# Scale steps, compressed scores and output products of a two-layer decoder trunk: which engine does them, and at which place in its order

## The chip, the cores and the metric

The kernel runs on one core of a Trainium2 chip. The metric is the device time of one execution in microseconds. A core has TensorE (PE: matmuls and transposes, with weight loads of their own), VectorE (DVE), ScalarE (ACT), GpSimd (POOL) and SyncE (SP, whose queue starts the transfers here). Each works through its own instruction stream in order; an instruction waits at its place until its operands are there, and what stands behind it on that engine waits too.

## The reference

Two layers over x of 1024 rows by 1024, each `x = x + (mixer(rmsnorm(x)) * silu(z)) @ w_out`, and a final rmsnorm. There are 16 heads of 64.

- Layer 0: full causal attention with a forget bias. `logits = q k^T / 8 + c[query] - c[key]`, with c the running sum of log sigmoids.
- Layer 1: three branches with 4 key and value groups, summed with gates. Compressed: 63 blocks of 32 keys (stride 16) go through a small MLP; `p_c` is the softmax over them, and `o_c = p_c v_c`. Chosen: the sums of p_c pick 8 of 16 blocks of 64 keys per query. Window: the last 512 keys.
- `o = g0 * o_c + g1 * o_s + g2 * o_w`, times silu(z), then `@ w_out`.

All is float32; the kernel keeps that precision by splitting operands into a high and a low part and adding up three products.

## The kernel before

**Order of the work.** The program is written as Python generators. `merge` interleaves a main generator (attention) with a filler (projections, output products) by costs that they yield and a ratio. That fixes the order in which instructions are traced. A scheduler then orders each engine's stream at compile time, by that order and by when it expects operands to be there, so an instruction traced late can be put earlier on its engine. `tc.keep_in_program_order(ins)` ties an instruction behind the last one traced before it on its engine.

**Layer 0.** `fox_main` runs score, softmax and value products for head pairs p = 0 to 7. `fox_fill` projects k, v, q, z of the next pair (`fox_k`, `fox_v`, `fox_q`, `fox_z`; each in two halves of 512 tokens, 8 steps of three matmuls a half). `early.step`, called once in each half, loads one piece of a later weight and has ACT sum its squares into a column of `sums`; columns 49 to 64 belong to `fox_w_out`. Power-of-two scales come out of such sums: `roots` (L187) copies the columns to bf16 on ACT, multiplies with ones on PE (tile `total_...`), and reduces and shifts exponents on DVE. `z_scale(p)` (L578) does it for z, `out_scales` (L226) for the output product: its first `roots` takes the square of the largest entry of `ao`, its second the sums of W_out. With the scale at hand `load_wout16` (L678) splits four rows of 128 of W_out into float16 halves: ACT the high part, DVE (L695) or POOL (L697, L698) the low part. `out_start0` then starts the output product in the filler. Where a pair's last super tile ends, its output is transposed and multiplied with z.

**Layer 1, projections and compressed branch.** `cmp_main` handles 16 units (`cmp_unit`, L1304: group g, half s, u: two tiles of 128 queries times four heads). The compressed keys `kcm` are held as high and low part side by side. Eight matmuls (L1310) write 128 columns each, high and low scores, into a tile `sc` of two banks, of which there is one buffer. DVE adds low part and mask (L1321, twice), then the high part (L1323), takes the minimum (L1324); ACT makes eight exponentials into `Pc` (L1326); DVE normalises, and for s = 1 sums over the heads (`pcs`, L1336) and picks blocks; POOL multiplies `Pc` in place with the gates (L1340). PE later transposes it (`ptc`, L1367). Meanwhile `nsa_fill` projects.

**Layer 1, attention.** `NsaSuper` is one head and one half s: eight `unit`s (y = 0 chosen, y = 1 window; four query tiles). A unit's scores (L1632) go to one of two buffers of two banks; DVE adds the mask and takes the minimum `m` in one instruction (L1640); for the window, DVE turns it into the exponent's offset (L1642); ACT makes the exponentials (L1643). Window probabilities are split on POOL (L1646, L1647) and transposed by DMA; chosen ones are transposed on PE (L1665) and split by ACT and DVE (L273, L274). `close` (L1713) transposes a pair's output, adds the compressed branch (L1723) and multiplies with the scale `ready["c", p]` and z (L1724), all on DVE; ACT and POOL split the product (L1731). The filler is `nsa_zs`: z projections (`nsa_z`), with `nz_scale(p - 1)` (L1448) four steps into the next, `limits` (L1432) once, then `out_scales`, the split of W_out and `out_start`. `out_rest` ends the program.

Of the kernel before, what the change touches and what calls it, by code (L numbers as in the profile page):

```python
# [25 lines left out]
GR = 4  # L26
# [15 lines left out]
def tile_fox_nsa(ctx, tc, a, out):  # L42
# [28 lines left out]
    tri = consts.tile([P, P], F32, name="tri")  # L71
    eps = consts.tile([P, 1], F32, name="eps")
# [153 lines left out]
    def out_scales(ao, cols, name, u, pool):  # L226


        V.tensor_reduce(u[:, 8:9], ao, AX.X, OP.max)
        V.tensor_tensor(u[:, 9:10], u[:, 8:9], u[:, 8:9], OP.mult)  # L230
        r = roots(u[:, 9:10], ((0, 1),), f"{name}a", pool)
        w = roots(cols, ((0, cols.shape[1]),), f"{name}w", pool)
        V.tensor_scalar(u[:, 10:11], r[:, 1], 2.0 ** 70, None, OP.mult)
        V.tensor_scalar(u[:, 11:12], w[:, 1], 2.0 ** 69, None, OP.mult)
        V.tensor_scalar(u[:, 0:8], ao, u[:, 10:11], None, OP.mult)
        V.tensor_scalar(u[:, 0:8], u[:, 0:8], u[:, 11:12], None, OP.mult)
        V.tensor_scalar(u[:, 10:11], r[:, 0], 2.0 ** 58, None, OP.mult)
        V.tensor_scalar(u[:, 11:12], w[:, 0], 2.0 ** 57, None, OP.mult)
        V.tensor_tensor(u[:, 10:11], u[:, 10:11], u[:, 11:12], OP.mult)
        return u[:, 0:8], u[:, 10:11]  # L240
# [323 lines left out]
    def fox_z(p, w, halves=(1, 0)):  # L564
# [3 lines left out]
        zs["q"] = zq = sb[0].tile([P, 6], F32, tag="zq", bufs=3, name=f"zq_{p}")  # L568
# [9 lines left out]
    def z_scale(p):  # L578
# [3 lines left out]
        V.tensor_tensor(zq[:, 2:3], zq[:, 0:1], zq[:, 1:2], OP.add)  # L582
# [5 lines left out]
    early = Squares(sa, [(a["nsa_w"][i][:, 4 * x:4 * x + 4, :], 2 * n + x)  # L588
                         for n, i in enumerate((*range(12), *range(20, 28))) for x in range(2)]
                    + row_sets(a["fox_w_out"], 512, 49)  # L590
# [5 lines left out]
    def fox_fill():  # L596
        for p in range(8):
            if p >= 2:
                yield lambda p=p: ("scored", p - 2) in ready
            yield from k0 if p == 0 else fox_k(p)  # L600
# [12 lines left out]
            else:  # L613
                wq, wz = next_w(), next_w()
                yield from fox_z(p, wz)
                yield from fox_q(p, wq, (1,))
                z_scale(p)
                rows0 = load_wout16(hp, "fox_w_out", 1, 200)
                yield next(rows0)
                last_q = fox_q(p, wq, (0,))  # L620
                for _ in range(4):
                    yield next(last_q)
                assert len(early.at) == 1 and not early.items
                ready["wscale"], ready["undo"] = out_scales(ao[0], sums[:, 49:65], "o0", un0, sb[0])
# [836 lines left out]
    def nsa_z(p, w, halves=(1, 0)):  # L1461
        if p == 0:
            limits()
# [411 lines left out]
```

## Time and profile before

| what | value |
|---|---|
| median of three runs | 1459.39 us (1457.80 to 1462.68) |
| profiled execution | 1460.85 us |
| its span, first to last instruction | 1458.8 us |
| mean granted clock of TensorE | 0.986 |
| busy: PE, DVE, ACT, POOL | 1364.8, 1119.4, 915.7, 588.2 us |

Busy time of PE counts overlapping matmuls once. The profile's windows give each engine's busy time in a stretch of the span, and the granted clock there (1.00 is full speed). In rows of waits the first engine and line waited for the second, with the total in us, the number of times and the longest. A bracket behind a timeline row is the idle time of the engine just ahead, and what ended it.

### The profile page before, as it was taken

The numbers are of one execution on the slowest core, as the hardware profiler recorded it, in microseconds if no ns is written. First come the engines' busy times: TensorE is split into PE (matmuls) and PEld (weight loads), VectorE is DVE, ScalarE is ACT, GpSimd is POOL, SyncE is SP. The second block draws the span as 40 slices with busy tenths as digits, with TensorE's granted clock in tenths as the row PEclk, the third lists the DMA queues.
The fourth block names the chain that finished last, engine by engine and source line by source line (L and its number), as shares of the span: only waits on it lengthen the run. The fifth ranks groups of instructions, "written<-read, shape, count | busy, mean of one in ns | idle before, by whom it ended". The sixth has DMA issues, their size and how long they took to land. (4 is left out here: it accounts for less than half of the span.)

```text
span 1458.8 us, 30392 instructions
## 1 busy us (share of the span) xinstructions
PE 1364.8 (94%) x10499; PEld 928.3 (64%) x10499; DVE 1119.4 (77%) x3018; ACT 915.7 (63%) x2328; POOL 588.2 (40%) x785
## 2 busy tenths in 40 slices
PE   5999999999999989989999987979999999988998
PEld 4878888888888745445545543446666767666643
DVE  6586777787877798586757667878989999989834
ACT  5376667776766665155554575657778787777512
POOL 2242433434243261221204455246756676654500
PEclk9999999999999999999999999999999999999999
DMA  5388898988989999354655447454767776785534
GB/s 202 91 176 183 198 186 184 215 184 191 193 196 186 230 235 207 115 174 139 188 179 149 130 123 159 117 140 95 135 151 169 128 177 119 146 182 108 106 109 144
DMA packets 414922, 234.72 MB, mean 161 GB/s; under 512 B 334448, under 2 KB 372656, under 8 KB 414768
## 3 DMA queue, kind: packets, MB, share of 16 engines
q1 hardware_dynamic: 414768, 232.78, 67.8%
q8 instruction: 83, 1.36, 0.4%
q14 instruction: 71, 0.58, 0.1%
HBM read 120.31 MB, written 28.38 MB: 102 GB/s over the span
## 5 line engine op out<-in xcount | busy, mean ns | idle before, releaser
L1632 PE MATMUL S_n<-nk,nq 128*128 128x320 f16 (+5 forms) x768 | 155.9, 316 | 20.7 <-DVE m_n L1640 16.1
L766 ACT ACTIVATE P<-P,m 128x512 f32<-128x512 f32 (+1 forms) x192 | 116.3, 606 | 54.6 <-DVE m L757 53.4
L1647 POOL TENSOR_TENSOR hl_n<-P_n,hl_n 128x640 f16<-128x640 f32 (+4 forms) x128 | 144.3, 1127 | 10.0
L737 POOL TENSOR_TENSOR Bd<-B,tri 128x128 f32<-128x128 f32 x128 | 61.5, 496 | 201.0 <-DVE m L757 190.1
L768 DVE SCALAR_TENSOR_TENSOR hl<-P,hl 128x512 f16<-128x512 f32 (+1 forms) x192 | 116.2, 621 | 26.4 <-ACT hl L767 25.1
L1646 POOL CAST hl_n<-P_n 128x640 f16<-128x640 f32 (+4 forms) x128 | 75.1, 587 | 126.9 <-ACT P_n L1643 102.4
L1643 ACT ACTIVATE P_n<-P_n,m_n 128x640 f32<-128x640 f32 (+7 forms) x128 | 98.5, 770 | 31.5 <-DVE m_n L1640 30.8
L1643 ACT ACTIVATE P_n<-P_n,m_n,units 128x640 f32<-128x640 f32 (+4 forms) x128 | 100.1, 782 | 24.5 <-DVE m_n L1642 23.8
L1632 PEld LDWEIGHTS <-nq 128*128 128x128 f16 x768 | 71.9, 98 | 67.9 <-issue 28.6
L273 ACT ACTIVATE pth_n<-ptp_n 128x512 f16<-128x512 f32 (+1 forms) x160 | 85.2, 545 | 44.4 <-PE ptp_n L1665 43.8
L274 DVE SCALAR_TENSOR_TENSOR ptl_n<-ptp_n,pth_n 128x512 f16<-128x512 f32 (+1 forms) x160 | 99.8, 633 | 11.8 <-ACT pth_n L273 10.0
L1665 PE MATMUL ptp_n<-ident,P_n 128*128 128x128 f32 x576 | 96.1, 285 | 5.8 <-ACT P_n L1643 1.6
L767 ACT ACTIVATE hl<-P 128x512 f16<-128x512 f32 (+1 forms) x192 | 92.5, 513 | 1.6 <-DMA pT<-hl 0.2
L1640 DVE CUSTOM_DVE_ANT_0 P_n<-S_n,wmask 128x640 f32<-128x640 f32 (+4 forms) x128 | 83.2, 650 | 6.4 <-PE S_n L1632 6.0
L1665 PEld LDWEIGHTS ptp_n<-ident,P_n 128*128 128x128 f32 x576 | 66.7, 144 | 29.8 <-DVE ptl_n L274 10.2
L183 ACT ACTIVATE sq<-sq,zg 128x512 f32<-128x512 f32 (+2 forms) x73 | 59.5, 815 | 25.3 <-DMA sq<-in_fox_w_out_dram 14.7
L1673 PE MATMUL O_n<-nv,pth_n 128*128 128x64 f16 x576 | 72.3, 194 | 0.3
L1674 PE MATMUL O_n<-nv,pth_n 128*128 128x64 f16 x576 | 72.2, 194 | 0.0
L97 ACT ACTIVATE h_n<-xr 128x512 f32<-128x512 f32 x32 | 20.0, 626 | 81.6 <-DVE xr L1765 39.2
L1640 DVE CUSTOM_DVE_ANT_0 P_n<-S_n,bias,units 128x640 f32<-128x640 f32 (+1 forms) x64 | 68.8, 1075 | 3.0 <-PE S_n L1632 2.8
L1675 PE MATMUL O_n<-nv,ptl_n 128*128 128x64 f16 x576 | 69.2, 194 | 0.1
L748 PE MATMUL S<-KH,Q 128*128 128x512 f32 (+1 forms) x192 | 65.2, 355 | 0.7 <-DVE m L757 0.7
(520 smaller groups left out, 4727.1 us busy)
## 6 DMA issues: line engine op xcount, KB each, us to landing
sq<-in_nsa_w_dram SPq DMA_DIRECT2D x40, 256.0 KB
B<-cD SPq DMA_DIRECT2D x16, 512.0 KB
nq<-qD SPq DMA_DIRECT2D x64, 128.0 KB
x<-in_x_dram SPq DMA_DIRECT2D x8, 512.0 KB
wst_k<-in_fox_w_dram SPq DMA_DIRECT2D x8, 512.0 KB
wst_v<-in_fox_w_dram SPq DMA_DIRECT2D x8, 512.0 KB
wst_q<-in_fox_w_dram SPq DMA_DIRECT2D x8, 512.0 KB
KH<-KH SPq DMA_DIRECT2D x32, 128.0 KB
```

Of the source, the lines that this page charges most:

```text
L273: A.activation(hi[:, 0:n], pt[:, 0:n], AF.Copy, scale=scale)
L274: V.scalar_tensor_tensor(lo[:, 0:n], pt[:, 0:n], scale, h, OP.mult, OP.subtract)
L766: A.activation(L[:, 0:n], L[:, 0:n], AF.Exp, bias=init, scale=-1.0, accum_out=self.lr[:, col + c:col + c + 1])
L767: A.activation(hi[:, cs], L[:, 0:n], AF.Copy, scale=UP)
L768: V.scalar_tensor_tensor(lo[:, cs], L[:, 0:n], UP, hi[:, cs], OP.mult, OP.subtract)
L1632: T.matmul(ps[:, b, 0:w], self.q[x][:, qi * P:(qi + 1) * P], k[:, k0 + b * w:k0 + b * w + w], start=(x == 0), stop=(x == 1))
L1640: V.tensor_tensor_reduce(dst, src, mk, 1.0 if y else unit, 3e38, OP.add, OP.min, m)
L1643: A.activation(L, L, AF.Exp, bias=m, scale=minus if y else -1.0, accum_out=self.l[:, y, qi:qi + 1])
L1646: G.tensor_copy(hl[:, 0:n], L)
L1647: G.tensor_tensor(hl[:, n:2 * n], L, hl[:, 0:n], OP.subtract)
L1665: T.transpose(pt[:, (x + i) * P:(x + i + 1) * P], L[:, kb * P - k0:(kb + 1) * P - k0], ident)
L1673: T.matmul(o, hi, v[:, 0:64], start=first, stop=False)
```

## The change

Seven things are done.

1. `out_scales` is cut into `w_scale` (sums of W_out), `out_scales1` (largest entry, squared by ACT, multiplied with ones on PE) and `out_scales2` (the rest, on DVE). In layer 0 `w_scale` runs at p = 3; for this the pieces of `fox_w_out` are the first in the list of `early`. In layer 1 it runs in `limits2`.
2. The first DVE instruction of `z_scale`, `nz_scale`, `limits2` and `out_scales2` is kept in program order; `limits` is cut in two, with the second part four steps into the next half.
3. For p = 7 of layer 0 the order is z half 1, q half 1, loads of W_out, z half 0, two steps of q half 0, `z_scale`, `out_scales1`, four steps, `out_scales2`, the rest. Of that half of W_out, DVE does two of four rows whole (`vrows`); the other halves stay as they were.
4. `cmp_unit`: sixteen matmuls of 64 columns add high and low part in one bank (two buffers); one DVE instruction adds the mask; exponentials stay in `L`, and POOL writes `Pc` from it.
5. The offset of the window's minimum is made by ACT (Identity, with bias `lnup`).
6. `nz_scale` has ACT scale z in place, and `close` multiplies with z on POOL.
7. In layer 1 the yields around `out_scales` are 1500 and 2500 in place of 2000.

The diff, with little of its context:

```diff
@@ -69,6 +69,8 @@
     tri = consts.tile([P, P], F32, name="tri")
+    lnup = consts.tile([P, 1], F32, name="lnup")
+    G.memset(lnup, LNUP)
     eps = consts.tile([P, 1], F32, name="eps")
@@ -223,21 +225,34 @@
-    def out_scales(ao, cols, name, u, pool):
+    late_on = tc.keep_in_program_order
+
+    def w_scale(cols, name, pool):
+
+
+        r = roots(cols, ((0, cols.shape[1]),), name, pool)
+        V.tensor_scalar(r[:, 2], r[:, 0], 2.0 ** 57, None, OP.mult)
+        V.tensor_scalar(r[:, 3], r[:, 1], 2.0 ** 69, None, OP.mult)
+        return r
+
+    def out_scales1(ao, u, name, pool):
...
         V.tensor_reduce(u[:, 8:9], ao, AX.X, OP.max)
-        V.tensor_tensor(u[:, 9:10], u[:, 8:9], u[:, 8:9], OP.mult)
-        r = roots(u[:, 9:10], ((0, 1),), f"{name}a", pool)
-        w = roots(cols, ((0, cols.shape[1]),), f"{name}w", pool)
-        V.tensor_scalar(u[:, 10:11], r[:, 1], 2.0 ** 70, None, OP.mult)
-        V.tensor_scalar(u[:, 11:12], w[:, 1], 2.0 ** 69, None, OP.mult)
+        tb = pool.tile([P, 1], BF16, name=f"sb_{name}")
+        A.activation(tb, u[:, 8:9], AF.Square)
+        pt = ps_t(f"total_{name}")
+        T.matmul(pt[:, 0:1], ones, tb, start=True, stop=True)
+        return pt
+
+    def out_scales2(ao, u, pt, w):
+        late_on(V.tensor_copy(u[:, 8:9], pt[:, 0:1]))
+        half_root(u, 8)
+        V.tensor_scalar(u[:, 10:11], u[:, 10:11], 2.0 ** 70, None, OP.mult)
         V.tensor_scalar(u[:, 0:8], ao, u[:, 10:11], None, OP.mult)
-        V.tensor_scalar(u[:, 0:8], u[:, 0:8], u[:, 11:12], None, OP.mult)
-        V.tensor_scalar(u[:, 10:11], r[:, 0], 2.0 ** 58, None, OP.mult)
-        V.tensor_scalar(u[:, 11:12], w[:, 0], 2.0 ** 57, None, OP.mult)
-        V.tensor_tensor(u[:, 10:11], u[:, 10:11], u[:, 11:12], OP.mult)
-        return u[:, 0:8], u[:, 10:11]
+        V.tensor_scalar(u[:, 0:8], u[:, 0:8], w[:, 3], None, OP.mult)
+        V.scalar_tensor_tensor(u[:, 11:12], u[:, 9:10], 2.0 ** 58, w[:, 2], OP.mult, OP.mult)
+        ready["wscale"], ready["undo"] = u[:, 0:8], u[:, 11:12]
@@ -565,7 +580,9 @@
             ao.append(sb[0].tile([P, 8], F32, name="ao0", bufs=1))
-        zs["q"] = zq = sb[0].tile([P, 6], F32, tag="zq", bufs=3, name=f"zq_{p}")
+        if "q" not in zs:
+            zs["q"] = sb[0].tile([P, 6], F32, tag="zq", bufs=3, name=f"zq_{p}")
+        zq = zs["q"]
         for half in halves:
@@ -579,15 +596,14 @@
         zq = ready["zt", p]["q"]
-        V.tensor_tensor(zq[:, 2:3], zq[:, 0:1], zq[:, 1:2], OP.add)
+        late_on(V.tensor_tensor(zq[:, 2:3], zq[:, 0:1], zq[:, 1:2], OP.add))
         half_root(zq, 2)
...
-    early = Squares(sa, [(a["nsa_w"][i][:, 4 * x:4 * x + 4, :], 2 * n + x)
+    early = Squares(sa, row_sets(a["fox_w_out"], 512, 49) + [(a["nsa_w"][i][:, 4 * x:4 * x + 4, :], 2 * n + x)
                          for n, i in enumerate((*range(12), *range(20, 28))) for x in range(2)]
-                    + row_sets(a["fox_w_out"], 512, 49)
                     + [(a["nsa_w_g"].rearrange("(k p) c -> p k c", p=P), 40)], 512, 1)
@@ -597,6 +613,8 @@
                 yield lambda p=p: ("scored", p - 2) in ready
+            if p == 3:
+                wr0 = w_scale(sums[:, 49:65], "o0w", sb[0])
             yield from k0 if p == 0 else fox_k(p)
@@ -612,22 +630,25 @@
                 wq, wz = next_w(), next_w()
-                yield from fox_z(p, wz)
+                yield from fox_z(p, wz, (1,))
                 yield from fox_q(p, wq, (1,))
+                rows0 = load_wout16(hp, "fox_w_out", 1, 200, 2)
+                yield next(rows0)
+                yield from fox_z(p, wz, (0,))
+                last_q = fox_q(p, wq, (0,))
+                for _ in range(2):
+                    yield next(last_q)
                 z_scale(p)
-                rows0 = load_wout16(hp, "fox_w_out", 1, 200)
-                yield next(rows0)
-                last_q = fox_q(p, wq, (0,))
+                pt = out_scales1(ao[0], un0, "o0", sb[0])
                 for _ in range(4):
                     yield next(last_q)
-                assert len(early.at) == 1 and not early.items
-                ready["wscale"], ready["undo"] = out_scales(ao[0], sums[:, 49:65], "o0", un0, sb[0])
+                out_scales2(ao[0], un0, pt, wr0)
                 yield from last_q
...
                 ready["o7"] = hp.tile([P, NT, 2, P], F16, tag="h11", name="o7_0")
-                yield from out_start0(load_wout16(hp, "fox_w_out", 0, 200))
+                yield from out_start0(load_wout16(hp, "fox_w_out", 0, 200, 0))
@@ -675,7 +696,7 @@
-    def load_wout16(pool, src, half, pace, gp=True):
+    def load_wout16(pool, src, half, pace, vrows):
@@ -691,7 +712,7 @@
                 A.activation(w[:, 0, k, cs], lo[:, k, cs], AF.Copy, scale=sc)
-                if c or not gp:
+                if c or k < vrows:
                     V.scalar_tensor_tensor(w[:, 1, k, cs], lo[:, k, cs], sc, w[:, 0, k, cs], OP.mult, OP.subtract)
@@ -955,7 +976,7 @@
     psP = tc.alloc_tile_pool(name="psP", bufs=2, space=PSUM, reuse_waits="tile")
-    psC = tc.alloc_tile_pool(name="psC", bufs=1, space=PSUM, reuse_waits="tile")
+    psC = tc.alloc_tile_pool(name="psC", bufs=2, space=PSUM, reuse_waits="tile")
@@ -1304,40 +1325,38 @@
         kcm = ready["kcm"]
-        sc = psC.tile([P, 2, 512], F32, tag="sc", name=f"sc_{nm}")
+        sc = psC.tile([P, 4, 2, 64], F32, tag="sc", name=f"sc_{nm}")
         for y in range(2):
             for r in range(4):
-                T.matmul(sc[:, y, r * P:(r + 1) * P], Q[r][:, (2 * u + y) * P:(2 * u + y + 1) * P],
-                         kcm[:, g].rearrange("p a c -> p (a c)"), start=True, stop=True)
-        sc = sc.rearrange("p y (r a c) -> p y r a c", r=4, a=2)
+                for x in range(2):
+                    T.matmul(sc[:, r, y], Q[r][:, (2 * u + y) * P:(2 * u + y + 1) * P], kcm[:, g, x],
+                             start=(x == 0), stop=(x == 1))
         t0 = 4 * s + 2 * u
-        L = pc[0].tile([P, 2, 4, 64], F32, tag="cL", bufs=2, name=f"cL_{nm}")
+        L = pc[0].tile([P, 4, 2, 64], F32, tag="cL", bufs=2, name=f"cL_{nm}")
         Pc = pc[0].tile([P, 2, 4, 64], F32, tag="cP", bufs=4, name=f"cP_{nm}")
         sm = pc[0].tile([P, 3, 8], F32, tag="cs", bufs=3, name=f"cs_{nm}")
-        L8 = L.rearrange("p y r c -> p (y r) c")
-        P8 = Pc.rearrange("p y r c -> p (y r) c")
+        L8 = L.rearrange("p r y c -> p (r y) c")
         uc = ready["uc"]
-        for y in range(2):
-            V.scalar_tensor_tensor(L[:, y], sc[:, y, :, 1, :], uc, cmask[:, t0 + y, None, :].to_broadcast([P, 4, 64]),
-                                   OP.mult, OP.add)
-        V.scalar_tensor_tensor(L8, sc.rearrange("p y r a c -> p (y r) a c")[:, :, 0, :], uc, L8, OP.mult, OP.add)
+        mk = cmask[:, t0:t0 + 2].rearrange("p y c -> p (y c)")[:, None, :].to_broadcast([P, 4, 128])
+        V.scalar_tensor_tensor(L.rearrange("p r y c -> p r (y c)"), sc.rearrange("p r y c -> p r (y c)"), uc, mk,
+                               OP.mult, OP.add)
         V.tensor_reduce(sm[:, 0, :], L8, AX.X, OP.min)
         for i in range(8):
-            A.activation(P8[:, i, :], L8[:, i, :], AF.Exp, bias=sm[:, 0, i:i + 1], scale=-1.0, accum_out=sm[:, 1, i:i + 1])
+            A.activation(L8[:, i, :], L8[:, i, :], AF.Exp, bias=sm[:, 0, i:i + 1], scale=-1.0, accum_out=sm[:, 1, i:i + 1])
         V.reciprocal(sm[:, 2, :], sm[:, 1, :])
+        ri = sm[:, 2, :].rearrange("p (r y) -> p r y", y=2)
         if t0 == 0:
-            V.tensor_scalar(sm[:, 2, 0:4], sm[:, 2, 0:4], crow, None, OP.mult)
-        ri = sm[:, 2, :].rearrange("p (y r) -> p y r", y=2)
+            V.tensor_scalar(ri[:, :, 0], ri[:, :, 0], crow, None, OP.mult)
         gc = gates[:, t0:t0 + 2, 12 * g:12 * g + 12:3]
         if s:
-            V.tensor_tensor(P8, P8, sm[:, 2, :, None].to_broadcast([P, 8, 64]), OP.mult)
+            V.tensor_tensor(L8, L8, sm[:, 2, :, None].to_broadcast([P, 8, 64]), OP.mult)
             pcs = pc[0].tile([P, 2, 65], F32, tag="pcs", bufs=2, name=f"pcs_{nm}")
             G.memset(pcs[:, :, 0:1], 0.0)
-            V.tensor_reduce(pcs[:, :, 1:65], Pc.rearrange("p y r c -> p y c r"), AX.X, OP.add)
+            V.tensor_reduce(pcs[:, :, 1:65], L.rearrange("p r y c -> p y c r"), AX.X, OP.add)
         else:
-            V.tensor_tensor(ri, ri, gc, OP.mult)
-            gc = ri
-        G.tensor_tensor(Pc, Pc, gc[:, :, :, None].to_broadcast([P, 2, 4, 64]), OP.mult)
+            V.tensor_tensor(ri, ri, gc.rearrange("p y r -> p r y"), OP.mult)
+            gc = ri.rearrange("p r y -> p y r")
+        G.tensor_tensor(Pc, L.rearrange("p r y c -> p y r c"), gc[:, :, :, None].to_broadcast([P, 2, 4, 64]), OP.mult)
         if s:
@@ -1429,7 +1448,7 @@
-    def limits():
+    def limits1():
@@ -1437,30 +1456,37 @@
             T.matmul(pt[:, g:g + 1], va[:, g, :], ones[:, 0:1], start=True, stop=True)
+        return pt
+
+    def limits2(pt):
         b = pers.tile([P, 2, GR], F32, name="limits")
-        V.tensor_scalar(b[:, 0], pt[:, 0:GR], ready["units"][2], None, OP.mult)
+        late_on(V.tensor_scalar(b[:, 0], pt[:, 0:GR], ready["units"][2], None, OP.mult))
         V.scalar_tensor_tensor(b[:, 0], vinv, 2.0 ** 16, b[:, 0], OP.mult, OP.add)
...
         ready["limits"] = b[:, 1]
+        ready["w1"] = w_scale(late.out, "o1w", pers)
...
         zq = ready["zt", p]["q"]
-        V.tensor_tensor(zq[:, 2:3], zq[:, 0:1], zq[:, 1:2], OP.add)
+        late_on(V.tensor_tensor(zq[:, 2:3], zq[:, 0:1], zq[:, 1:2], OP.add))
         half_root(zq, 2)
...
         V.tensor_scalar(ao1[:, p:p + 1], zq[:, 7:8], 0.5, None, OP.mult)
-        ready["c", p] = zq[:, 6:7]
+        for half in (1, 0):
+            z = ready["zt", p][half]
+            A.activation(z, z, AF.Copy, scale=zq[:, 6:7])
+        ready["c", p] = True
...
         if p == 0:
-            limits()
+            sums_v = limits1()
         zs = ready.setdefault(("zt", p), {})
@@ -1472,6 +1498,11 @@
                 nz_scale(p - 1)
+            if not half and not p:
+                for _ in range(4):
+                    yield next(steps)
+                assert not late.items and not late.at
+                limits2(sums_v)
             yield from steps
@@ -1482,18 +1513,20 @@
             if p == 6:
-                rows0 = load_wout16(h1, "nsa_w_out", 1, 400, False)
+                rows0 = load_wout16(h1, "nsa_w_out", 1, 400, 4)
                 yield next(rows0)
...
             yield from nsa_z(p, zw[p])
-        assert not late.items and not late.at
-        yield 2000
+        yield 1500
         nz_scale(7)
-        ready["wscale"], ready["undo"] = out_scales(ao1, late.out, "o1", pers.tile([P, 12], F32, name="un1"), pers)
+        un1 = pers.tile([P, 12], F32, name="un1")
+        pt = out_scales1(ao1, un1, "o1", pers)
+        yield 2500
+        out_scales2(ao1, un1, pt, ready["w1"])
         yield from rows0
         ready["o7"] = h1.tile([P, NT, 2, P], F16, tag="h11", name="o7_1")
-        yield from out_start(load_wout16(h1, "nsa_w_out", 0, 400, False))
+        yield from out_start(load_wout16(h1, "nsa_w_out", 0, 400, 4))
@@ -1639,7 +1672,7 @@
             if y:
-                V.tensor_scalar(m, m, unit, LNUP, OP.mult, OP.add)
+                A.activation(m, m, AF.Identity, bias=lnup, scale=unit)
             A.activation(L, L, AF.Exp, bias=m, scale=minus if y else -1.0, accum_out=self.l[:, y, qi:qi + 1])
@@ -1721,7 +1754,7 @@
             V.scalar_tensor_tensor(o, pt, vinv[:, self.g:self.g + 1], o, OP.mult, OP.add)
-            V.scalar_tensor_tensor(o, o, ready["c", p], ready["z", p, s][s], OP.mult, OP.mult)
+            G.tensor_tensor(o, o, ready["z", p, s][s], OP.mult)
             if p == 7:
```

## The prediction

> **What bounds the kernel now.** I read the page's engine totals first, then the waits of TensorE, then windows by stage, then the timeline around the longest gaps.
>
> ```profile
> span 1458.8 us, 30392 instructions
> PE 1364.8 (94%) x10499; PEld 928.3 (64%) x10499; DVE 1119.4 (77%) x3018; ACT 915.7 (63%) x2328; POOL 588.2 (40%) x785
> ```
>
> TensorE (PE) is the bound as a whole: 94.0 of 1458.8 us are without a matmul. The change takes no matmul work away, so it can only win from those 94 us, and from slow-clock time behind gaps. The windows say where they lie (columns: window, length, busy time of PE, weight loads, DVE, ACT, POOL, granted clock, DMA share, GB/s):
>
> ```profile
> 505.00:515.00 10.00, 7.08 (x50) 5.40 (x50) 8.40 (x34) 6.58 (x18) 1.13 (x3) 0.83 1.12 287
> 515.00:545.00 30.00, 23.70 (x141) 11.87 (x138) 28.43 (x68) 19.61 (x47) 22.46 (x24) 0.94 0.96 235
> 800.00:950.00 150.00, 133.86 (x744) 71.33 (x742) 108.16 (x267) 92.32 (x349) 67.40 (x97) 0.99 0.50 130
> 950.00:975.00 25.00, 18.10 (x88) 9.46 (x89) 17.02 (x59) 14.16 (x29) 11.87 (x14) 0.91 0.58 166
> 1116.00:1166.00 50.00, 48.05 (x623) 34.14 (x621) 46.08 (x128) 39.42 (x93) 35.08 (x42) 1.00 0.81 168
> 1300.00:1335.00 35.00, 27.22 (x338) 20.11 (x336) 30.43 (x94) 28.52 (x62) 14.95 (x19) 0.90 0.60 132
> ```
>
> PE is idle 9.2 us where layer 0 ends (505 to 545), 16.1 in the compressed branch (800 to 950), 6.9 where attention of layer 1 starts (950 to 975), 2.0 per 50 us inside attention, 7.8 where its output scales are made (1300 to 1335). The waits name what ended those gaps (us in total, times, longest):
>
> ```profile
> PE S_n L1632 <- DVE m_n L1640: 16.1, 24, 2.8
> PE ptc_c L1367 <- POOL cP L1340: 6.5, 5, 2.2
> PE ptc_c L1367 <- POOL pcs L1335: 5.4, 2, 3.3
> PE S_n L1632 <- DMA nq<-qD: 3.7, 1, 3.7
> PE sc L1310 <- DVE cL L1323: 3.5, 1, 3.5
> PE y L257 <- POOL wo_fox_w_out L698: 3.5, 3, 1.6
> POOL cP L1340 <- DVE pcs L1336: 17.2, 3, 7.0
> ```
>
> **Part A, the end of layer 0.** The timeline, with the idle time ahead in brackets:
>
> ```profile
> 504.73 0.18 PE L196 MATMUL total_o0a<-sb_o0a,ones 128*128 128x1 bf16 x1
> 509.33 0.17 PE L196 MATMUL total_o0w<-sb_o0w,ones 128*128 128x16 bf16 x1 [2.92 <-ACT sb_o0w L194]
> L698 POOL TENSOR_TENSOR wo_fox_w_out<-wos_fox_w_out,wo_fox_w_out x8: 1154/1314/1532, 515.7 to 537.5; 128x512 f16<-128x512 f32 x8
> L697 POOL TENSOR_SCALAR wos_fox_w_out<-wos_fox_w_out,un x8: 692/918/1230, 514.8 to 536.8; 128x512 f32<-128x512 f32 x8
> L695 DVE SCALAR_TENSOR_TENSOR wo_fox_w_out<-wos_fox_w_out,un,wo_fox_w_out x8: 737/772/1650, 515.3 to 541.0; 128x512 f16<-128x512 f32 x8
> ```
>
> The sum over the squares of fox_w_out (total_o0w) holds the in-order PE for 2.92 us, because its last squares come last in the list of loads. The diff puts them first and sums them at p = 3: the 2.92 us go. The window 505 to 515 runs at a clock of 0.83, which on 7.08 us of matmuls is 1.2 us more; that goes with the gap. The new sum at p = 3 can wait for its own squares: between 0 (total_o0a did not wait) and 2.9; near the first, since 17 squares should be done by then: +0.5. The Square and matmul of out_scales1 stand where total_o0a stood, four steps of the last query projection ahead of their use; a wait there is again between 0 and 2.9, and I take 0, as the row shows. Behind that wait every matmul would queue.
>
> Of the first half of W_out, two of four rows go from POOL to DVE. POOL loses 2 x (0.92 + 1.31) = 4.5 us, DVE gains 2 x 0.77 = 1.5. PE waited 3.5 us on these POOL instructions; the later rows also come earlier, so I take 2.0 of it. DVE is busy 28.43 of 30 us in that window, and scores queue behind the added 1.5: between 0 and 1.5, I take 0.6. Four weight DMAs (128 x 1024 each) are issued one projection sooner on SP's queue, past the load of one set of squares and the transposes of the attention ahead; if they delay those, ACT waits in its square and its exponentials queue behind it. The moved loads took the same queue before, so I take 0. Bounds for all of A: -8 (both waits and both slow stretches gone) and +3 (one new 2.9 us wait). Sum: -2.9 - 1.2 - 2.0 + 0.5 + 0.6 = **-5.0**. What is late next is the DVE itself.
>
> **Part B, pinned scale steps.** In the timeline of DVE and PE at the start of attention:
>
> ```profile
> 960.73 0.16 DVE L1452 TENSOR_TENSOR nzq<-nzq 128x1 f32<-128x1 f32 x1 [6.12 <-ACT nz L1477]
> 962.79 1.84 PE L1632 MATMUL S_n<-nk,nq 128*128 128x384 f16 x8 [2.82 <-DVE m_n L1640]
> ```
>
> The scheduler put the first instruction of nz_scale(0) ahead of the mask set-up and the first scores; it held the in-order DVE 6.12 us for ACT, and PE then ran out of score banks. The pin puts it behind what was traced before it, so the first minima can start some 5 us sooner. The window's idle PE time is 6.9 us, so the gain is between 0 (something else is late: ACT is idle only 10.8 of 25 us) and 6.9; I take **-4.0**, a little more than the named gap of 2.82, as the following short waits of the same kind lie in the same window. The later nz_scale steps did not wait so long; pinning them costs nothing as long as their use is a pair of heads later. limits split in two, and w_scale of layer 1 (one bf16 copy on ACT, one matmul, some 0.15 us instructions on DVE), lie under the projection of z of p = 0.
>
> **Part C, the compressed scores.** Rows by line (minimum/median/maximum ns), and two pieces of the timeline:
>
> ```profile
> L1321 DVE SCALAR_TENSOR_TENSOR cL<-sc,rc,cmask x32: 431/474/484, 822.6 to 942.6; 128x256 f32<-128x256 f32 x32
> L1323 DVE SCALAR_TENSOR_TENSOR cL<-sc,rc,cL x16: 699/750/753, 823.5 to 943.4; 128x512 f32<-128x512 f32 x16
> L1336 DVE TENSOR_REDUCE pcs<-cP x8: 1023/1039/1056, 834.8 to 948.7; 128x128 f32<-128x512 f32 x8
> 910.74 0.62 PE L1310 MATMUL sc<-kcm,nq 128*128 128x128 f16 x8 [3.55 <-DVE cL L1323]
> 1104.22 0.19 PE L1673 MATMUL O_n<-nv,pth_n 128*128 128x64 f16 x1
> 1104.54 0.19 PE L1675 MATMUL O_n<-nv,ptl_n 128*128 128x64 f16 x1
> ```
>
> On PE, 8 matmuls of 128 columns become 16 of 64, each with its own weight load. The eight take 0.62 us. Twelve 64-column matmuls start within 1104.22 to 1104.54, 0.029 apart, so sixteen take some 0.47 plus a tail of 0.16: nothing lost. On DVE, per unit, 2 x 0.474 + 0.750 becomes one of about 0.750: 0.95 less, 16 units, 15.2 us in all. The exponentials now stay in L, so POOL's product with the gates no longer waits until the sum pcs (1.04 us, 8 units) has read its operand; that wait is most of POOL's 17.2 us. So the chain that ends in the transposes ptc is 0.95 to 2.0 us shorter per unit. Seven waits there cost PE 6.5 + 5.4 us, 1.7 each, so at most 11.9 go; the second score bank takes away the 3.5 us wait of sc. Upper bound 15.4, lower bound 0 (the interleaving with projections fixes the pace, and the next projection's operand may be late instead). I take a third, **-5.0**, as DVE and ACT are busy only 72% and 62% there, which leaves room, but ptc waits also hang on ACT's eight exponentials, which stay.
>
> **Part D, attention of layer 1.** Groups by shape and line:
>
> ```profile
> L1642 DVE TENSOR_SCALAR m_n<-m_n,units 128x1 f32<-128x1 f32 x128 | 26.3, 206 | 1.2
> L984 ACT ACTIVATE zr<-pn_qr,roots_early 128x1 f32<-128x1 f32 x6 | 1.6, 259 | 4.2 <-DVE spl_qr L1151 4.2
> L1724 DVE SCALAR_TENSOR_TENSOR no<-no,nzq,nz 128x512 f32<-128x512 f32 x16 | 14.1, 879 | 0.1
> L1731 POOL TENSOR_TENSOR ot_n<-no,ot_n 128x512 f16<-128x512 f32 x14 | 16.2, 1160 | 2.9 <-ACT ot_n L1730 2.9
> L1232 ACT ACTIVATE nvT<-nvT,nvsc x8: 706/712/723, 852.0 to 889.4; 128x512 f32<-128x512 f32 x8
> L1454 DVE TENSOR_SCALAR nzq<-nzq x8: 141/153/155, 965.8 to 1306.5; 128x1 f32<-128x1 f32 x8
> L1455 DVE TENSOR_TENSOR nzq<-nzq,limits x8: 148/474/883, 968.8 to 1309.4; 128x1 f32<-128x1 f32 x8
> ```
>
> DVE loses 128 steps on the minima (26.3 us) and 16 products (14.1 us): 40.4 us of the some 430 between 960 and 1390, from 92% busy (46.08 of 50) to about 83%. ACT gains 128 x 0.259 = 33.2 us (L984 is the nearest form: Identity on one column with a bias from SBUF) and two scalings of z per pair, 16 x 0.712 = 11.4 us: 44.6 us, from 79% (39.42 of 50) to about 89%. POOL gains 16 x 1.16 = 18.6 us, from 70% to 74%. So the load changes sides rather than going away: the minimum's step stays in the chain from score to exponential, 0.259 in place of 0.206, and what queues behind a late minimum is now ACT's queue, the copies pth among it, not DVE's. PE is idle 2.0 of 50 us, 430/50 x 2.0 = 17 us over the stage, 5 to 7 of them already in part B. Bounds: -9 (most of what is left) and +22 (two thirds of ACT's 33.2 exposed). I take **-1.5**, near the first end, since DVE is the fuller engine before and PE's waits name DVE's minimum. In the last pair POOL's 1.16 in place of DVE's 0.88 would add 0.3 us; the output products of row tiles 4 to 7, which need only the other half, cover it.
>
> L1455 and L1454 show that DVE instructions reading two SBUF tensors wait for something: both work on one column, one takes 148 to 883 ns, the other 155 at most. The Trainium skill, "SBUF — State Buffer", section "Who interferes with whom", says why: DVE and GpSimd share a port pair as an exclusive lock, and a DVE instruction with two SBUF inputs blocks against a GpSimd instruction that reads SBUF. By that rule the move to POOL has a price: six per cent more POOL time, and as much more of such waits. By the rows it takes one such DVE instruction (L1724) away for each product added, so the sum would be the same within 0.5 us. The trace agrees with the rule.
>
> **Part E, the scales of layer 1's output.** out_scales2 comes 2000 cost units of filler later, so the split of W_out starts 2 to 4 us later; the 3.7 us wait in the window 1300 to 1335 is one for a DMA of queries, which the change does not touch. Between -2 and +3; I take 0.
>
> **Sum.** -5.0 - 4.0 - 5.0 - 1.5 + 0 = -15.5 us against the profiled execution, 1460.85 us (its span of 1458.8 and 2.05 around it): 1445.3. The median of the three runs shown is 1459.39, 1.46 below the profiled one, so 1444 for the median.
>
> **The rivals.** Two more waits, of ACT's exponentials for their minima:
>
> ```profile
> ACT P_n L1643 <- DVE m_n L1640: 30.8, 50, 1.4
> ACT P_n L1643 <- DVE m_n L1642: 23.8, 38, 1.9
> ```
>
> First, slower: ACT becomes the bound in attention. Place: the wait of ACT's exponentials on their minimum (L1643), with the new one-column step in series. Price: two thirds of 33.2 us exposed, +22, against -14.0 from A to C: 1469. It decides above 42% exposed (14.0 / 33.2); for it speaks ACT at 89%, against it that ACT now idles 54.6 us for these minima, which a faster DVE shortens. Chance 0.08. Second, only the named holds go: total_o0w with its slow clock, and 2 us in B, while C and D return as other waits: -6, 1454 to 1455, chance 0.24; for it speaks that PE is nearly full everywhere. Third, the pins do not do it: the scheduler moves other early-ready steps ahead, or the new totals hold PE: -3 or less, 1457, chance 0.12. Fourth, relief reaches further: A -7, B -5, C -9, D -6: -27, 1433, chance 0.10. For it speaks that DVE's 55 us less is much more than I count.
>
> **How the numbers follow.** The forecast has 0.46. From 1433 to 1458 lie the forecast, the second rival, and half of the third and fourth: 0.81; the forecast's own range is 1438 to 1451. About 4.4 us (0.3%) is what a measurement can tell. Faster by more: 0.46 + 0.10 + most of 0.24 = 0.78; within: 0.12; slower: 0.10, the first rival and a little of the third.
>
> **What would show it.** A: no wait at total_o0w, a clock near 1.0 from 505 to 515. B: no long wait at the add of nz_scale(0), PE over 22 of 25 us. C: no POOL wait on pcs, none of PE on cL. D: ACT 87% or more, DVE under 86%, PE waits on m_n about half. Wrong if PE's waits name ACT's minimum or POOL's product more often than they named DVE's, or if a total of scales holds PE by more than 2 us.

## The result, and the profile after

The changed kernel takes 1469.52 us (median of five runs, 1468.47 to 1473.06), the kernel before 1460.26 (1457.80 to 1462.68). The ratio is 1.0062, with a 95% interval of 1.0046 to 1.0078: some 9 us slower. Forecast were 1444, and 1433 to 1458. The profiled execution took 1470.02 us. Its totals:

```profile
span 1468.2 us, 30569 instructions
PE 1367.2 (93%) x10627; PEld 929.9 (63%) x10627; DVE 1082.0 (74%) x2840; ACT 961.0 (65%) x2472; POOL 601.1 (41%) x798
```

Work moved as announced (DVE 37 us less, ACT 45 more), and PE, with the same work, is without a matmul for 101.0 us in place of 94.0. The start times of the same rows in both timelines show where: the first projection of layer 1 0.6 us later than before (641.16 and 640.59), the first score of its attention (`S_n`) 2.4 later (955.59, 953.22), the last row of output transposes `ptn` of the sixth pair 10.1 later (1277.05, 1266.93), the last of all 7.5 (1395.72, 1388.18), the end 9.4. So 2.4 us are lost ahead of the attention of layer 1, and the larger part in its pairs. The windows (columns as before), the last one pair of heads:

```profile
505.00:515.00 10.00, 8.11 (x42) 6.26 (x42) 6.04 (x25) 5.07 (x14) 0.91 (x2) 0.66 1.09 302
...
950.00:975.00 25.00, 18.41 (x98) 9.64 (x96) 18.38 (x56) 16.03 (x36) 10.77 (x13) 0.97 0.65 185
...
1120.00:1171.00 51.00, 48.05 (x620) 33.99 (x619) 42.79 (x108) 44.53 (x110) 36.64 (x45) 1.00 0.83 157
```

Before, a pair took 49.8 us (mean of four, 1067.77 to 1266.93), now 51.7 (1070.17 to 1277.05). ACT is busy 44.5 us of 51, DVE 42.8: they have changed places. The waits of PE over the whole run and, in attention (975 to 1385), of ACT:

```profile
PE S_n L1665 <- DVE m_n L1673: 13.0, 23, 1.8
PE total_o L245 <- ACT sb_o L243: 5.8, 2, 4.4
PE ptp_n L1698 <- DVE ptl_n L289: 5.6, 16, 0.9
PE O_n L1706 <- ACT pth_n L288: 5.5, 11, 1.5
PE ptp_n L1698 <- ACT P_n L1676: 5.3, 6, 1.6
...
ACT P_n L1676 <- DVE m_n L1673: 19.7, 21, 2.8
...
ACT ot_n L1763 <- POOL no L1757: 12.4, 14, 1.2
```

PE waits less for minima (16.1 before) and more for what comes out of ACT: copies `pth`, and `ptl` behind them. ACT itself waits less for minima: over the whole run its exponentials and the new step wait 25.6 us, where the exponentials waited 54.6. The last row is new: the f16 cast of the output product, on ACT, waits 14 times for POOL's product.

Of the runs below, the profiled execution of e4 ran at a granted clock of 0.85 (1551.71 us), and its profile is not read.

### The profile page after: what moved, and what is told of

Same layout as the page of the kernel before. It is cut to its first block, busy times and chain, and to the rows that moved or that the text cites. A ratio compares the mean times of both kernels' runs of the same rounds, so it can differ in the third digit from the quotient of the medians.

```text
span 1468.2 us, 30569 instructions
## 1 busy us (share of the span) xinstructions
PE 1367.2 (93%) x10627; PEld 929.9 (63%) x10627; DVE 1082.0 (74%) x2840; ACT 961.0 (65%) x2472; POOL 601.1 (41%) x798
## 5 line engine op out<-in xcount | busy, mean ns | idle before, releaser
L1680 POOL TENSOR_TENSOR hl_n<-P_n,hl_n 128x640 f16<-128x640 f32 (+4 forms) x128 | 140.9, 1101 | 9.5
```

The costliest lines, as they stand in the source:

```text
L1680: G.tensor_tensor(hl[:, n:2 * n], L, hl[:, 0:n], OP.subtract)
```

## The experiments

All numbers are medians; the kernel before had 1460.1 to 1460.7 in these comparisons. "Pair" is the time per pair of heads in the profile, from the same four pairs as above; "tie" is ACT's wait for POOL's product in attention.

| kernel | us | ratio to before, 95% | pair | tie |
|---|---|---|---|---|
| changed | 1469.5 | 1.0046 to 1.0078 | 51.7 | 12.4 |
| e1: minima back on DVE | 1460.15 | 0.9989 to 1.0014 | 50.1 | 11.8 |
| e2: z back on DVE | 1457.51 | 0.9974 to 0.9998 | 49.8 | none |
| e3: both back | 1453.70 | 0.9943 to 0.9971 | 49.6 | none |
| e4: before, minima on ACT | 1460.22 | 0.9989 to 1.0012 | | |
| f1: changed, z scaled by DVE | 1470.95 | 1.0058 to 1.0084 | 52.6 | 15.5 |
| f2: changed, product on DVE | 1460.62 | 0.9993 to 1.0015 | 50.2 | none |
| f3: e1 with idle activations | 1466.24 | 1.0023 to 1.0051 | 50.9 | 13.0 |
| g1: e3 without pins | 1451.19 | 0.9931 to 0.9954 | 49.8 | none |
| h1: changed, cast on POOL | 1460.83 | 0.9990 to 1.0019 | 50.5 | none |
| h2: changed, cast later | 1468.66 | 1.0039 to 1.0077 | 51.3 | none |
| g2: g1 with the old scores | 1454.80 | 0.9940 to 0.9971 | 49.8 | none |
| g3: before, new scores | 1455.89 | 0.9952 to 0.9979 | 49.8 | none |
| i1: f2 with a dead POOL product | 1464.15 | 1.0018 to 1.0044 | 50.5 | none |
| i2: the same, tied | 1489.01 | 1.0186 to 1.0227 | 55.2 | 26.1 |
| k1: before, pins on `nz_scale` | 1456.92 | 0.9971 to 0.9990 | 49.5 | none |
| b3: g1, z, product and cast on POOL | 1443.74 | 0.9872 to 0.9906 | 49.1 | none |
| c1: b3 with the pins | 1450.72 | 0.9926 to 0.9958 | 48.9 | none |
| c2: b3 with minima on ACT | 1451.10 | 0.9926 to 0.9955 | 49.9 | none |

**The two edits in attention.**

```diff
e1, e3:
-                A.activation(m, m, AF.Identity, bias=lnup, scale=unit)
+                V.tensor_scalar(m, m, unit, LNUP, OP.mult, OP.add)
e2, e3:
-            G.tensor_tensor(o, o, ready["z", p, s][s], OP.mult)
+            V.scalar_tensor_tensor(o, o, ready["c", p], ready["z", p, s][s], OP.mult, OP.mult)
-            A.activation(z, z, AF.Copy, scale=zq[:, 6:7])   (twice a pair)
```

> The changed kernel with one thing put back: the scale and offset of the near minima on DVE. Theory M (this one-column step, 0.377 us each on ACT where the prediction counted 0.259, in series between score and exponential on an engine that is busy 44.5 of 51.6 us per pair of heads, is what lengthens the pair from 49.7 to 51.6): 1460 to 1462, a pair of heads back at 49.3 to 49.9. Theory Z (the product with z on GpSimd, 1.27 us each in front of the f16 splits that feed the transposing DMAs, and z's scaling on ACT, are what does it): 1467 to 1470. Theory L (both together, by the load they put on ACT, 48.3 + 11.4 us): 1462 to 1464.

> The changed kernel with the other thing put back: outputs times z as one product on DVE that takes the scale along, no scaling of z on ACT. Theory M: 1467 to 1470, as the minima stay on ACT. Theory Z: 1460 to 1462. Theory L: 1465 to 1468, about a fifth of the loss (11.4 of 59.7 us of ACT's added work).

> Both put back, so that the end of layer 0, the pinned scale steps and the compressed scores stay changed. If these three parts bring nothing of the 14 us predicted for them, as the two traces suggest (both start attention at the same time within 0.8 us): 1458 to 1461 under each of the theories M, Z and L. If they bring what was predicted and attention loses it: 1446. If the loss is not in attention's two edits at all but in a pinned step or in a changed order: 1466 to 1470.

> The kernel before with one thing of the change: the scale and offset of the near minima on ACT. Theory M: 1467 to 1470, pairs of heads of 51 to 52 us. Theory Z: 1459 to 1461. Theory L: 1465 to 1467.

None of the three theories holds by itself. From e3 the minima on ACT cost 3.8 us (e2), z moved away costs 6.5 (e1), both cost 15.8: 5.5 more than their sum. In the kernel before, the minima's step costs nothing that can be measured (e4). And the rest of the change gains 6.7 us, half of the 14.0 forecast for A to C. The profiled execution of e3 took 1460.53 us, well above its median, so only attention is read from its profile.

**Load, chain or product.**

```diff
f1:
-            A.activation(z, z, AF.Copy, scale=zq[:, 6:7])
+            V.tensor_scalar(z, z, zq[:, 6:7], None, OP.mult)
f2:
-            G.tensor_tensor(o, o, ready["z", p, s][s], OP.mult)
+            V.tensor_tensor(o, o, ready["z", p, s][s], OP.mult)
f3, on e1, ahead of each window exponential:
+                A.activation(md, lnup, AF.Identity, bias=lnup, scale=unit)
```

> The changed kernel with z scaled by DVE and not by ACT (16 instructions of 128x512); minima on ACT and the product on GpSimd stay. So far: the change 1469.5, minima alone on ACT 1457.5, z alone moved 1460.2, neither 1453.7. Theory L (ACT has too much work in sum; the last of it costs most): 11.4 of ACT's 59.7 added us go, 1459 to 1463. Theory Q (the product on GpSimd, 1.27 us in front of the f16 splits, meets the later exponentials): 1467 to 1470.

> The changed kernel with the product with z back on DVE; z is still scaled by ACT, the minima are on ACT. Theory L: ACT keeps all of its work, 1466 to 1470. Theory Q: 1457 to 1460.

> The changed kernel with the minima's step on DVE, and beside it for each near score one more one-column activation on ACT that reads constants only and whose result nobody uses: ACT's load of the change without its step in the chain from score to exponential. Without the extra activations this was 1460.2, the change 1469.5. Theory L: 1467 to 1472, the load does it wherever it stands. Theory C (the longer chain, 0.377 for 0.206 us in series): 1460 to 1462.

Taking 11 us of z's scaling from ACT gains nothing (f1; DVE has that work instead, and the tie grows to 15.5), taking the product from POOL gains 9 (f2). In f3 idle activations, outside the chain, cost 6.1 of the 9.4 us that the minima's step costs in that company. So load on ACT counts there, inside the chain or not. It counts without the product on POOL too: f2, with the minima and z's scaling on ACT, is 6.9 us above e3. In the waits of these kernels one row goes with the loss: ACT's cast for POOL's product, 12 to 16 us wherever the product is on POOL with its cast on ACT. That gave theory W.

**The tie between the queues.**

```diff
h1:
-            A.copy(ot[:, :, 0], o4)
+            G.tensor_copy(ot[:, :, 0], o4)
h2: the A.copy pinned some seven instructions later in ACT's stream
i1, on f2, behind the product on DVE:
+            G.tensor_tensor(dead, o, ready["z", p, s][s], OP.mult)
i2, in its place:
+            G.tensor_tensor(o, o, one, OP.mult)
```

> The changed kernel with the f16 cast of the product (128x512, 16 times) moved from ACT to GpSimd, right behind the product. Theory W (new: the cast stands in ACT's queue and waits for GpSimd's product, 14 times for 12.4 us in all, and exponentials queue behind it; with the product on DVE this wait was 0 to 0.6 us): the wait cannot occur, 1457 to 1461, although GpSimd has 16 more instructions. Theory Q (the work on GpSimd in front of the f16 splits is what costs): GpSimd has still more of it, 1469 to 1474.

> The changed kernel with every instruction left on its engine; only the f16 cast of the product stands seven places later in ACT's queue (after two or three more exponentials), and the subtraction behind it on GpSimd accordingly later. Theory W: the product is done when ACT gets there, the wait of 12.4 us falls below 3 and the time to 1459 to 1463. Theory Q: 1468 to 1471.

> The kernel with only the product put back on DVE (1460.6 so far), and one more product of outputs and z on GpSimd behind it, 16 times, into a tile that nobody reads: GpSimd has the work of the change, at the same place in its queue, and ACT's cast waits for DVE alone. Theory W (what costs is that ACT's cast has to wait for GpSimd's queue): 1459 to 1462. Theory Q (GpSimd's work in front of the f16 splits costs): 1467 to 1470.

> As the last one, with the same number and size of instructions on each engine, but GpSimd's extra product is one of the outputs with a tile of ones, in place, so that ACT's cast has to wait for it. Theory W: the wait of ACT for GpSimd is back with some 12 us, 1467 to 1470. Theory Q: the same time as the last one, whichever it is.

h1 gives POOL still more work and is 8.7 us faster; the rest of the compiled order is nearly that of the change (of the 5016 matmuls from the first score to the last `ptn` 24 stand elsewhere, on POOL two rows). It also takes 10 us of casts from ACT; f1 took 11 and gained nothing, but gave them to DVE, so h1 alone does not tell the tie from ACT's load. h2 is a miss for W: the wait is gone and the time is not. But there some 350 of the matmuls changed places, POOL waits 7.1 us for ACT's late cast instead, and PE 7.6 for `pth`, so it does not decide against W either. i1 and i2 decide: the same number of instructions, in almost the same order (i1 that of f2 with the products added; against i1, 35 of the 5016 matmuls and 16 of ACT's 894 rows moved in i2), and the tie is the difference that is left. Both miss W's numbers: i1 lies between the two theories, and i2's wait (26.1 us) is twice what W had said, its time 19 us more.

The waits of ACT in attention, i1 first, then i2, and one pair of i2 around the tie (POOL, ACT, PE):

```profile
ACT pth_n L288 <- PE ptp_n L1698: 20.5, 24, 4.9
ACT P_n L1676 <- DVE m_n L1673: 18.8, 30, 1.5
```

```profile
ACT ot_n L1767 <- POOL no L1761: 26.1, 14, 3.8
ACT pth_n L288 <- PE ptp_n L1701: 19.8, 19, 5.0
ACT P_n L1679 <- DVE m_n L1676: 16.9, 25, 1.5
...
PE ptp_n L1701 <- ACT P_n L1679: 13.4, 10, 2.0
```

```profile
1188.45 1.73 POOL L1683 TENSOR_TENSOR hl_n<-P_n,hl_n 128x640 f16<-128x640 f32 x1
1190.14 1.27 POOL L1761 TENSOR_TENSOR no<-no,one 128x512 f32<-128x512 f32 x1
...
1191.44 0.62 ACT L1767 CAST ot_n<-no 128x512 f16<-128x512 f32 x1 [2.31 <-POOL no L1761]
1192.38 0.92 ACT L1679 ACTIVATE P_n<-P_n,m_n,units 128x640 f32<-128x640 f32 x1
...
1193.30 1.13 ACT L1679 ACTIVATE P_n<-P_n,m_n 128x1024 f32<-128x1024 f32 x1
...
1194.58 0.44 PE L1701 MATMUL ptp_n<-ident,P_n 128*128 128x128 f32 x2 [2.04 <-ACT P_n L1679]
```

POOL has its product behind a split of window probabilities (1.73 us). ACT comes to its cast and stands still for 2.31 us; the exponentials behind it come late; PE reaches the transposes of their result and waits 2.04 us. The split that POOL does is itself fed by ACT's exponentials, so the two queues hold each other. That the tie costs is shown: 24.9 us between i1 and i2. In the change, without a DVE product ahead, the wait is half as long. What it costs there can be read by adding one thing at a time to e3 (1453.70): the minima on ACT 3.8 (e2), z's scaling on ACT 3.1 (f2), a product on POOL that nobody reads 3.5 (i1), and the tie, with DVE's product gone, 5.4 (the change). Each step is a difference between medians of separate comparisons, known to 2 or 3 us. So theory Q and ACT's load have parts of their own beside W.

**The other parts.**

```diff
g1, on e3:
-    late_on = tc.keep_in_program_order
+    late_on = lambda x: x
g2, on g1: cmp_unit and psC as before
g3, on the kernel before: cmp_unit and psC as changed
k1, on the kernel before, in nz_scale:
-        V.tensor_tensor(zq[:, 2:3], zq[:, 0:1], zq[:, 1:2], OP.add)
+        tc.keep_in_program_order(V.tensor_tensor(zq[:, 2:3], zq[:, 0:1], zq[:, 1:2], OP.add))
```

> The kernel with both attention edits put back (1453.7), and the pins of the scale steps taken away as well. If the pins are what brings the 6.7 us below the kernel before: 1458 to 1461. If the gain is from the end of layer 0, from the compressed scores, or from the output scales' new place: 1453 to 1455. My reading of the profiles: the end of layer 0 and the compressed scores bring nothing (they start attention within a microsecond), some 1.5 us come at the first scale step, 2 over the pairs, 3.7 at the end of attention.

> The kernel with both attention edits put back and no pins (1451.2), and the compressed scores as they were before, with their one bank. If the compressed scores bring the 5 us that were predicted: 1456. If they bring nothing, as the profiles suggest (from the first compressed score to the first near score 131 to 134 us with and without): 1450 to 1453.

> The kernel before with the compressed scores and their second bank alone. As predicted for this part: 1455. If they bring nothing: 1459 to 1461.

> The kernel before with the first instruction of each of the eight scale steps of layer 1 pinned, nothing else. As predicted (part B): 1455 to 1457, as the 6.12 us hold of DVE at the start of attention goes. If a pin makes the step late instead and what DVE would have waited for is late all the same, as in the comparison of the kernels with and without pins (1453.7 and 1451.2): 1460 to 1463.

My reading of the first profiles, that the compressed scores bring nothing, was wrong: alone they gain 4.8 us (g3), and 3.6 in the company of the rest (g1 against g2). The end of layer 0 and the new output scales without pins gain 5.9 (g2). The pin alone gains 3.2 (k1, ratio 0.9971 to 0.9990), but taking all pins from e3 did not lose: 1451.2 against 1453.7, with intervals that overlap. The first DVE add of `nz_scale(0)` in g3, then k1, then the same row in the change, and the first PE gaps at the start of attention in g3:

```profile
961.46 0.25 DVE L1450 TENSOR_TENSOR nzq<-nzq 128x1 f32<-128x1 f32 x1
```

```profile
986.13 0.71 DVE L1452 TENSOR_TENSOR nzq<-nzq 128x1 f32<-128x1 f32 x1
```

```profile
990.91 1.39 DVE L1475 TENSOR_TENSOR nzq<-nzq 128x1 f32<-128x1 f32 x1
```

```profile
959.88 0.33 PE L1663 MATMUL ptp_n<-ident,P_n 128*128 128x128 f32 x1 [1.11 <-ACT P_n L1641]
...
960.85 1.46 PE L1630 MATMUL S_n<-nk,nq 128*128 128x448 f16 x8 [0.53 <-DVE m_n L1638]
```

In g3 nothing is pinned, and yet the add comes without its hold of 6.12 us, and the gap of 2.82 us is not there: with fewer DVE instructions ahead, the scheduler put the add behind the first minima (in the compiled order of the kernel before it stands ahead of the masks and of all minima). With the old scores and no pins the gap stays (2.83 us in g2). So B and C each remove the same gap. With C there, a pin only makes the step some 30 us later (990.91 for 961.46).

**The version that follows.** If the tie is the cost, the product belongs on POOL with all that hangs on it.

```diff
b3, on g1:
-            V.scalar_tensor_tensor(o, o, ready["c", p], ready["z", p, s][s], OP.mult, OP.mult)
+            G.tensor_scalar(ready["z", p, s][s], ready["z", p, s][s], ready["c", p], 1.0, OP.mult, OP.mult)
+            G.tensor_tensor(o, o, ready["z", p, s][s], OP.mult)
-            A.copy(ot[:, :, 0], o4)
+            G.tensor_copy(ot[:, :, 0], o4)
c1, on b3: the pins; c2, on b3: the minima on ACT
```

> A candidate: the version without pins and with the minima on DVE (1451.2), where GpSimd takes z's scaling, the product and the cast, so that ACT waits for none of it: DVE has 14 us less, ACT 10 us less, GpSimd some 46 us more (70 to 80% busy in attention). If the tie between the queues is what made GpSimd expensive: 1445 to 1450. If GpSimd's work itself delays the f16 splits: 1453 to 1460.

> The best version so far (1443.7: no pins, minima on DVE, all work with z on GpSimd) with the pins of the change. If the pins help as they did in the kernel before alone (-2.8): 1440 to 1442. If they cost as in the comparison of the two kernels with both attention edits put back (1453.7 with, 1451.2 without): 1445 to 1448.

> The best version so far with the minima's scale and offset on ACT, as in the change; ACT no longer waits for GpSimd's product. If the step on ACT costs by itself, as much as where z was all on DVE (3.8): 1446 to 1449. If it cost only together with the tie: 1442 to 1445. If it costs as much as it did with the tie (9.3): 1452.

b3 takes 1443.74 us, 0.9889 of the kernel before (0.9872 to 0.9906), the best of all. The window of one pair, and POOL's groups in it (busy us, mean ns, idle time ahead) for the three steps:

```profile
1106.00:1155.00 49.00, 47.45 (x622) 34.27 (x619) 43.70 (x124) 38.62 (x90) 39.25 (x48) 1.00 0.80 163
```

```profile
L1755 POOL TENSOR_TENSOR no<-no,nz 128x512 f32<-128x512 f32 x2 | 2.6, 1279 | 0.0
...
L1754 POOL TENSOR_SCALAR nz<-nz,nzq 128x512 f32<-128x512 f32 x2 | 1.4, 692 | 0.3 <-DVE nzq L1479 0.3
L1761 POOL CAST ot_n<-no 128x512 f16<-128x512 f32 x2 | 1.2, 616 | 0.1
```

POOL is busy 80% of the pair, more than in the change (72%), and does no harm: in attention ACT waits for it once, 1.2 us. From there the pins cost 7.0 us (c1) and the minima on ACT 7.4 (c2): ACT, at 38.6 of 49 us, has idle time left, and yet with the step, at 43.0 of 51, pairs are 0.8 us longer.

For the pins c1 shows the place too. The first instruction of `out_scales2` at the end of layer 0, in b3, then in c1:

```profile
505.86 0.16 DVE L249 COPY un<-total_o 128x1 f32<-128x1 f32 x1
```

```profile
514.06 0.15 DVE L249 COPY un<-total_o 128x1 f32<-128x1 f32 x1
```

The total is there at 506 in b3 and at 508 in c1; pinned, the copy comes at its place some 6 us later still, the scales of W_out with it, and the first output product starts at 518.5 in place of 514.4. The change has this row at 514.09 and starts at 518.6.

## Why the prediction was wrong, point by point

**A, -5.0: near in size without the pins, but by luck, and given back by them.** The wait at total_o0w went as said, and the new sum at p = 3 does not wait. "A wait there is again between 0 and 2.9, and I take 0" was mis-sized: `total_o` holds PE for 4.41 us, since z_scale itself ends at 506.3 and PE reaches the matmul at 502.5. That is also past the sign of being wrong that the prediction had named, 2 us. Nor is it the pins that do it. PE in g2, without pins, from 450 to 640 us:

```profile
PE total_o L245 <- ACT sb_o L243: 3.8, 1, 3.8
...
PE y L272 <- POOL wo_fox_w_out L719: 2.5, 2, 1.3
```

These are 6.3 us, where total_o0w and POOL's rows were 6.4 before. Yet layer 1 starts 5.0 us earlier in g2 (635.55 for 640.59), and 3.1 in g1 (637.53). From 515 to 545 the clock is 1.00 in both, 0.94 before; where the rest comes from is not settled. In the change POOL's wait fell to 0.4 us, the clock in 505 to 515 to 0.66 instead of rising, and the pins, priced at nothing, set the copy of `out_scales2` back 8 us: 2 by a later total, 6 by the copy's own place. Layer 1 starts 0.6 us late.

**B, -4.0: right alone (3.2), wrong in the sum.** The hold and the gap that were named are gone in k1. The failing step is that B and C were added up as if they removed different waits; both remove the one of 2.82 us. In company pins cost: 7.0 on b3; on e3 2.5, which is not clear of noise.

**C, -5.0: right in size (4.8), not in place.** In g3 the branch itself, from the first compressed score to the first `S_n`, is 1.7 us shorter (129.8 for 131.5); 5.0 come between there and the first `ptn` row (57.1 for 62.1), which was counted under B. PE's named waits, on `pcs` and on `cL`, are gone from the branch, and that on `cP` is 2.2 us less, but others came, on copies of ACT. PE in g3, from 800 to 955 us:

```profile
PE oc_c L256 <- ACT pth_c L270: 4.9, 2, 3.5
PE ptc_c L1365 <- POOL cP L1338: 4.3, 3, 3.0
PE pn_v L256 <- ACT nvT L1220: 3.0, 1, 3.0
```

**D, -1.5: the error.** It cost 15.8 us. The bounds, -9 to +22, held it; the value was taken near the wrong end, because DVE was the fuller engine. The first step that failed is the product's, 8.9 us (f2 against the change): its price was taken as 1.16 us of POOL in the last pair (it takes 1.27). Who waits behind it was not asked: the cast that follows was, and stayed, on ACT. Before, it waited for DVE 0.6 us in all; now it waits for an engine whose queue is full of splits, and exponentials stand behind it. The second is ACT's added time, 6.9 us (e3 against f2), and the minima's step in it. Its row of comparison was a form with one operand per partition:

```profile
L1675 ACT ACTIVATE m_n<-m_n,lnup,units x128: 370/377/405, 963.2 to 1384.4; 128x1 f32<-128x1 f32 x128
```

It takes 0.377 us, not 0.259, though an instruction right behind it starts 0.28 after it does, so ACT's time was nearly right. The Trainium skill, "ScalarE: Activation LUTs", section "What ACT_TABLE_LOAD costs", gives 186 ns for an activation with immediate scale and bias, some 93 more for each per-partition operand, and an overlap of some 93 between one activation and the next; with two such operands the estimate is 372 ns. The trace agrees. What failed is that ACT, at 89% by the forecast, would take this time almost free: the step alone costs 3.8 us on e3 and 7.4 on b3.

**The first rival has the number (1469; the profiled execution took 1470), but only half of the mechanism.** It put the loss at exponentials waiting for their minimum; that wait fell from 54.6 to some 26 us, the new step's own included. Its condition, ACT too full, is part of the cause (f2, f3, c2), but 5.4 of the 15.8 us have their place at the cast, which it did not name. **The second rival** (only named holds go, C returns: 1454 to 1455) is near what A, B, C and E give with the pins, 1453.7, but C did not return. **E, 0:** the wait of 3.7 us for queries is gone, the last two pairs are 2.6 us shorter (118.67 for 121.25), and the part after attention 1.9 longer, as 84 of the output product's 384 matmuls were done by then, and 93 before: -0.7, in pairs that D made longer.

Not settled: how e2 loses its 3.8 us, of which its pairs, 0.26 us longer than e3's, show some 2; where A's gain in g1 and g2 comes from; and why a step that is free in the kernel before (e4) is not free elsewhere.

## What to carry to other kernels

When an operation moves to another engine, list who reads its result and on which engine that reader stands: an in-order reader takes over the producer's backlog, and all that is behind it. Here it paid to move the chain up to its last link, or not at all: the same product on POOL cost 9 us with its cast on ACT and helped to gain 7 with all of it on POOL. Gains that rest on one gap are counted once, and a pin that cures a hold is to be tried again once another part has cured it.

## What the runs showed of the hardware that I had not expected

For 128x512 float32, POOL's scaling by a column takes 0.69 us and its cast to f16 0.62, half of its product of two tensors (1.28), and the cast is as fast as ACT's (0.62). So POOL, slow where two tensors are read, took three steps of this chain for 2.6 us.
